# Eighteen extra products on TensorE in a hybrid attention and RWKV-7 layer

## The chip, the cores and the metric

The kernel runs on one core of a Trainium2 chip. The metric is the device time of one execution in microseconds (us). Three runs of the kernel before took 785.77, 785.54 and 783.43 us, median 785.54. One more execution was profiled.

The engines are named as the profile names them: PE is TensorE's matmul, PEld its weight load, DVE is VectorE, ACT is ScalarE, POOL is GpSimd and SP is SyncE, which here only issues DMAs. PEq, SPq and the like are the sequencers of the engines. Each engine has its own list of instructions; where one of them is not ready, the trace shows the engine idle and names what ended the wait.

## The reference, cut to what matters

One transformer layer, 512 tokens of width 1024, all in fp32:

```python
proj = rmsnorm(x, ln_mix_g) @ w_in                   # 1024 x 3096
y_nsa  = nsa_mixer(proj[..., :1304], ...)            # attention: compressed, selected, window branch
y_rwkv = rwkv7_mixer(proj[..., 1304:], ...)          # a recurrent scan over 512 tokens, 8 heads of 64
x = x + concatenate([y_nsa, y_rwkv]) @ w_out
hidden = square(relu(rmsnorm(x, ln_ffn_g) @ w_ff1))  # 1024 x 4096
x = x + hidden @ w_ff2
```

The attention has 8 query heads in two groups of four; each group shares one key head. There are only 8 selectable blocks and up to 16 are taken, so the selected branch is plain causal attention over all 512 tokens, and so is the window branch. The end of the RWKV mixer that the change touches is

```python
g = sigmoid(xg) @ g2          # the output gate
y = (y + bonus * v) * g
```

## The kernel before, in words

Tokens are cut in four blocks of 128, counted by `i`. Large products are done as three products of a high and a low part (`mm3`, lines 332 to 334), with both parts in the type fp32r. Small products are plain fp32; the profile shows each of those as two matmul records, so that four products read as x8.

The work has these stages. First the input projection (tiles `pa`) runs, about 20 to 225 us. Woven into its second half and going on after it is the RWKV mixer, per block: `rw_prep` (decays, gates, the products `pg` at L586 and the transposes `ptb` at L597), `rw_inv` (the inverse of a triangular matrix by many 32x32 products `pz`, `pd`, `px`), `rw_vals`, `rw_chain` (the scan itself, tiles `pp`, `puu`, `py`, two steps a block) and `rw_out` (group norm, transposes `pty` at L787, the gate product `pgt` at L797, then `YR`). From about 230 us the attention runs beside it in eight units: `UNITS` holds group 0 with blocks 0 to 3, then group 1. For a unit, `attn_scores` makes the compressed scores `pcs` (L1053), then for each of two branches the scores `sc` (L1075) of four heads in one to four PSUM banks. DVE reads each bank with a fused add, minimum and row minimum (L1079), ACT takes the exponential (L1082), and DVE, ACT or POOL scale by the reciprocal sum. `attn_values` transposes the probabilities (`pT`, L1111) and multiplies with the values (`pv`). After about 384 us come the output projection and the feed-forward part, in which PE has long runs of `mm3`.

Three things set the order around the change. The generators of the stages are merged by a small planner (`merge`) that takes, of those ready, the one of highest priority, with made-up costs and delays in the `yield` lines. Then the tile framework schedules the recorded instructions with a timeline of its own, so that an added instruction may move others on every engine. Last, PSUM buffers are shared: `ps` has one buffer, which `pg`, `ptb`, `pty`, `pgt` and others take in turn, and `pa` has two, which `pcs` and the banks of `sc` take in turn. A product into a new tile waits until the old one has been read.

Other names of the change and the prediction: `ident` is the 128x128 unit matrix, `G2P` the permuted gate weights (128 x 512, fp32), `SG` the gate's input, `Qt` a unit's transposed queries (128 x 512, fp32r), `KT` the transposed keys, `QR` and `rs_yq` the queries of a group before their transposition and the reciprocal roots of their norms (a power on POOL, L302), `QU` the last part of the inverse.

Of the kernel before, what the change touches and what calls it, by code (L numbers as in the profile page):

```python
# [50 lines left out]
UNITS = [(i, g) for g in range(2) for i in range(NT)]  # L51
# [63 lines left out]
def layer(ctx: ExitStack, tc: tile.TileContext, A, cst, out):  # L115
    nc = tc.nc
    PSUM = bass.MemoryType.PSUM
    V, S, G, PE = nc.vector, nc.scalar, nc.gpsimd, nc.tensor

    def bc(ap, shape):  # L120
        return ap.to_broadcast(shape)
# [54 lines left out]
    def at(place, shape, name, dt=F32):  # L176
        size, n = PLACES[place]
        assert int(np.prod(shape[1:])) * 4 <= size
        return up.tile(shape, dt, name=name, tag=place, bufs=n)
# [10 lines left out]
    def small(n, name):  # L190
        return sm.tile([128, n], F32, name=name, tag=name, bufs=1 if n == 32 else 2)
# [12 lines left out]
    ident = identr.bitcast(F32)  # L204
# [13 lines left out]
    for q in FQ:  # L218
# [9 lines left out]
        else:  # L228
            h = int(q[1])
# [57 lines left out]
    def vec(key, j=0, n=1):  # L287
        return VEC[:, VO[key] + j:VO[key] + j + n]
# [10 lines left out]
    def rsqrt(v, n, key, p=128):  # L299

        y = small(n, "rs_y" + key)[0:p]
        G.tensor_tensor(y, v, bc(MH[0:p], [p, n]), op=ALU.pow)  # L302
        return y
# [27 lines left out]
    def mm3(o_, l, r, first, last):  # L331
        PE.matmul(o_, l[0], r[0], start=first, stop=False)  # L332
        PE.matmul(o_, l[0], r[1], start=False, stop=False)  # L333
        PE.matmul(o_, l[1], r[0], start=False, stop=last)  # L334

    def norm_T(i, x_, gain, NH_, NL_, place, pool, raw=None):

        ss = small(2, "ss")
        tmp = [at(place, [128, 512], "nt") for _ in range(2)]
        for b in range(2):  # L340
            S.activation(tmp[b], x_[b], AF.Square, scale=1.0 / 32, accum_out=ss[:, b:b + 1])
        vv = small(1, "vv")
        V.scalar_tensor_tensor(vv, ss[:, 0:1], 1e-6, ss[:, 1:2], op0=ALU.add, op1=ALU.add)
        rs = rsqrt(vv, 1, 'n')
        for b in range(2):
            V.scalar_tensor_tensor(tmp[b], x_[b], rs, gain[b], op0=ALU.mult, op1=ALU.mult)
            pt = pool([128, 4, 128], "pt")
            for kk in range(4):
                PE.transpose(pt[:, kk, :], tmp[b][:, kk * 128:(kk + 1) * 128], ident)
            S.copy(NH_[b][:, i], pt)  # L350
            if raw:
                S.copy(raw[b], pt)
            V.tensor_tensor(NL_[b][:, i], pt, NH_[b][:, i].bitcast(F32), op=ALU.subtract)
# [22 lines left out]
    G2P = at('c', [128, 4, 128], "G2P")  # L376
# [392 lines left out]
    def rw_out(i):  # L769
        st = ST[i]  # L770
        YY = st['YY']
        mean = small(8, "mean")
        V.tensor_reduce(mean, YY, axis=AX.X, op=ALU.add)
        V.tensor_scalar(mean, mean, 1.0 / 64, None, op0=ALU.mult)
        V.tensor_tensor(YY, YY, bc(mean.unsqueeze(2), [128, 8, 64]), op=ALU.subtract)
        sq = at('o', [128, 8, 64], "sqy")
        S.activation(sq, YY, AF.Square)
        var = small(8, "var")
        V.tensor_reduce(var, sq, axis=AX.X, op=ALU.add)
        V.tensor_scalar(var, var, 1.0 / 64, 64e-5, op0=ALU.mult, op1=ALU.add)  # L780
        rs = rsqrt(var, 8, 'o')
        V.tensor_tensor(YY, YY, bc(rs.unsqueeze(2), [128, 8, 64]), op=ALU.mult)
        yield 0.0, 5.0
        pt = ps([128, 2, 2, 2, 64], "pty")
        for c in range(2):
            for p in range(2):
                PE.transpose(pt[:, c, p].rearrange("p a b -> p (a b)"),  # L787
                             YY[:, 4 * c + 2 * p:4 * c + 2 * p + 2, :].rearrange("p a b -> p (a b)"), ident)
        Y1 = at('o', [128, 4, 128], "Y1")
        for p in range(2):  # L790
            for e in range(2):
                S.activation(Y1[:, 2 * p + e, :].rearrange("p (c t) -> p c t", c=2), pt[:, :, p, 1 - e, :],
                             AF.Identity, bias=vec('lnb', 2 * p + e), scale=vec('lnw', 2 * p + e))
        G.tensor_tensor(Y1, Y1, st['ZV'], op=ALU.add)
        pgt = ps([128, 4, 128], "pgt")
        for kt in range(4):
            PE.matmul(pgt[:, kt, :], G2P[:, kt, :], SG[:, i * 128:(i + 1) * 128], start=True, stop=True)  # L797
        YR[i] = at('zk', [128, 4, 128], "YR")
        V.tensor_tensor(YR[i], Y1, pgt, op=ALU.mult)
        done['out', i] = 1  # L800
        yield 1.3, 0.0
# [8 lines left out]
    def rw_outs():  # L810
        for i in range(NT):
            yield lambda: ('chain', i) in done
            yield from rw_out(i)
# [10 lines left out]
    KT, VH, QT = {}, {}, {}  # L824
# [211 lines left out]
    def gate_over(z, g_):  # L1036
        V.reciprocal(z, z)
        V.tensor_tensor(z, z, g_, op=ALU.mult)  # L1038
# [5 lines left out]
    def attn_scores(i, g):  # L1044
        yield lambda: (UNITS.index((i, g)) < 2 or ('attn',) + UNITS[UNITS.index((i, g)) - 2] in done) and all(k in done for k in ('gates', ('cmp', 0), ('cmp', 1), ('keys', 0), ('keys', 1), ('q', i, g)))
        w = (i + 1) * 128
        hb = max(1, 512 // w) if w != 384 else 1
        gts = GT[:, i].rearrange("p (h b) -> p b h", b=3)[:, :, 4 * g:4 * g + 4]
        Qt = QT[i, g]

        pcs = pa_([128, 4, 32], "pcs")
        for h in range(4):
            PE.matmul(pcs[:, h, :], Qt[:, h, :].bitcast(F32), KCT[:, g, :], start=True, stop=True)  # L1053
        pc = at('cs', [128, 4, 32], "pcm")
        mnc = small(4, "mnc")
        zc = small(4, "zc")
        for h in range(4):
            V.tensor_tensor_reduce(out=pc[:, h], in0=pcs[:, h], in1=CT2[:, C_CD + 32 * i:C_CD + 32 * i + 32],
                                   scale=2.0 ** -(4 * g + h + 1), scalar=3e38,
                                   op0=ALU.add, op1=ALU.min, accum_out=mnc[:, h:h + 1])  # L1060
            S.activation(pc[:, h], pc[:, h], AF.Exp, bias=mnc[:, h:h + 1], scale=-1.0, accum_out=zc[:, h:h + 1])
        gate_over(zc, gts[:, 0])
        V.tensor_tensor(pc, pc, bc(zc.unsqueeze(2), [128, 4, 32]), op=ALU.mult)
        yield 0.9, 0.0

        P = []
        for br in range(2):
            P_ = at('n8', [128, 4, 512], "P")
            mn = small(4, "mn")
            z = small(4, "z")  # L1070
            for h0 in range(0, 4, hb):
                sc = pa_([128, hb, w], "sc")
                for h in range(h0, h0 + hb):
                    for hl in range(2):
                        PE.matmul(sc[:, h - h0, :], Qt[:, h, :],  # L1075
                                  KT[br, g, hl].rearrange("p i t -> p (i t)")[:, 0:w], start=hl == 0, stop=hl == 1)
                for h in range(h0, h0 + hb):
                    p_ = P_[:, h, 0:w]
                    V.tensor_tensor_reduce(out=p_, in0=sc[:, h - h0, :], in1=DIST[:, 512 - w:512],  # L1079
                                           scale=2.0 ** -(4 * g + h + 1), scalar=3e38,  # L1080
                                           op0=ALU.add, op1=ALU.min, accum_out=mn[:, h:h + 1])
                    S.activation(p_, p_, AF.Exp, bias=mn[:, h:h + 1], scale=-1.0, accum_out=z[:, h:h + 1])  # L1082
                yield SCP * hb * w / 512, SCD * hb * w / 512
            gate_over(z, gts[:, 1 + br])
            for h in range(4):
                if (h, br) in SCA:
                    S.activation(P_[:, h, 0:w], P_[:, h, 0:w], AF.Copy, scale=z[:, h:h + 1])
                else:
                    (G if (h, br) in SCG else V).tensor_scalar(P_[:, h, 0:w], P_[:, h, 0:w], z[:, h:h + 1], None, op0=ALU.mult)  # L1089
            P.append(P_)  # L1090
        pct = pb_([128, 128], "pct")
        PE.transpose(pct, pc.rearrange("p h n -> p (h n)"), ident)
        pcT = at('cs', [128, 128], "pcT")
        S.copy(pcT, pct)
        AT[i, g] = P, pcT
        yield 0.9, 0.0
        done['sc', i, g] = 1
# [335 lines left out]
```

## Time and profile before

| what | value |
|---|---|
| median of three runs (lowest, highest) | 785.54 us (783.43, 785.77) |
| profiled execution | 783.81 us |
| its span, first to last instruction | 781.9 us |
| PE, PEld busy | 759.8 us (97%), 657.5 us (84%) |
| DVE, ACT, POOL busy | 511.8 us (65%), 395.6 us (51%), 175.2 us (22%) |
| mean granted clock of TensorE | 0.987 of full speed |
| chain of waits: PE, DVE, ACT, DMA | 84%, 7%, 4%, 3% of the span |

The span is 1.9 us shorter than the execution's time; the rest lies before the first and behind the last instruction. [...]

### The profile page before, as it was taken

Reading aid. Unit: us, or ns where it says so; the run is one execution under the profiler, and the core shown is the slowest. Engines: PE = TensorE matmul, PEld = TensorE weight load, DVE = VectorE, ACT = ScalarE, POOL = GpSimd, SP = SyncE. Lnnn points to the kernel's source line nnn. Section 1 sums busy time; section 2 is a strip of 40 time slices with the busy share of each in tenths; the row PEclk is TensorE's granted clock in tenths of the full one; section 3 lists DMA queues with packets and bytes.
Section 4 is the critical chain, followed back from the end, with each engine's and each line's share of the span. In section 5 each row is a group of like instructions: output and inputs, shape, how many; then the busy total and the mean of one; then the engine's idle time right before and its main releaser. Section 6 shows DMA issues by size and latency. Waiting matters only on the chain.

```text
span 781.9 us, 18278 instructions
## 1 busy us (share of the span) xinstructions
PE 759.8 (97%) x7357; PEld 657.5 (84%) x7357; DVE 511.8 (65%) x1157; ACT 395.6 (51%) x928; POOL 175.2 (22%) x176
## 2 busy tenths in 40 slices
PE   7999999999989999999999899999999999999998
PEld 5888888889879877887788899998888999978886
DVE  6444385585586789898755888973334989853333
ACT  7343433345444867888544655673332456653330
POOL 5002032240332353434400152300001323100000
PEclk9999999999985999999999999999999999999999
DMA  7741331111000000120343053233323433133212
GB/s 235 206 133 42 94 84 44 44 29 31 15 16 1 29 3 2 30 57 9 114 149 95 17 146 108 69 104 110 96 92 103 118 102 106 62 122 95 95 54 108
DMA packets 67338, 62.00 MB, mean 79 GB/s; under 512 B 6013, under 2 KB 53299, under 8 KB 67254
## 3 DMA queue, kind: packets, MB, share of 16 engines
q1 hardware_dynamic: 67254, 60.83, 25.9%
q8 instruction: 58, 0.95, 0.5%
q14 instruction: 26, 0.21, 0.1%
HBM read 58.72 MB, written 2.10 MB: 78 GB/s over the span
## 4 chain that ended last, share of the span: by engine, by line
PE 84%; DVE 7%; ACT 4%; DMA 3%; issue 1%; SPq 1%; POOL 0%; DVEq 0%; ACTq 0%; POOLq 0%
PE pa L332 8%; PE pa L333 8%; PE pa L334 8%; PE po L332 7%; PE po L333 7%; PE po L334 7%; PE pw L333 5%; PE pw L334 5%; PE pw L332 5%; PE pg L586 2%; PE sc L1075 2%; DMA wraw<-in_w_out_dram 1%; PE py L757 1%; PE pT L1111 1%; PE pz L681 1%
## 5 line engine op out<-in xcount | busy, mean ns | idle before, releaser
L311 ACT CAST whi<-wraw 128x512 fp32r<-128x512 f32 (+1 forms) x128 | 78.7, 622 | 133.4 <-PE po L333 29.1
L312 DVE TENSOR_TENSOR wlo<-wraw,whi 128x512 fp32r<-128x512 f32 (+1 forms) x120 | 86.7, 725 | 86.1 <-ACT whi L311 80.9
L332 PE MATMUL po<-whi 128*128 128x512 f32 x256 | 100.7, 394 | 1.2 <-DVE cc L1361 1.2
L333 PE MATMUL po<-wlo,whi 128*128 128x512 f32 x256 | 101.0, 395 | 0.0
L334 PE MATMUL po<-whi,wlo 128*128 128x512 f32 x256 | 100.7, 393 | 0.0
L333 PE MATMUL pw<-TT,whi 128*128 128x256 f32 x224 | 63.2, 282 | 0.0
L334 PE MATMUL pw<-TT,wlo 128*128 128x256 f32 x224 | 63.0, 281 | 0.0
L332 PE MATMUL pw<-TT,whi 128*128 128x256 f32 x224 | 62.5, 279 | 0.0
L332 PEld LDWEIGHTS po<-whi 128*128 128x128 f32 x256 | 48.0, 188 | 13.0 <-ACT whi L311 1.6
L334 PEld LDWEIGHTS po<-whi,wlo 128*128 128x128 f32 x256 | 48.1, 188 | 11.4
L333 PEld LDWEIGHTS po<-wlo,whi 128*128 128x128 f32 x256 | 48.0, 188 | 11.0
L332 PE MATMUL pa<-XH,whi 128*128 128x512 f32 (+1 forms) x144 | 53.0, 372 | 1.5 <-ACT XH L350 1.5
L333 PE MATMUL pa<-XL,whi 128*128 128x512 f32 (+1 forms) x144 | 53.7, 374 | 0.0
L334 PE MATMUL pa<-XH,wlo 128*128 128x512 f32 (+1 forms) x144 | 52.9, 370 | 0.0
L1291 POOL TENSOR_TENSOR ws<-wq 128x512 f32<-128x512 f32 x14 | 21.5, 1536 | 138.3 <-DMA wq<-in_w_ff_dram 123.2
L311 ACT CAST whi<-ws 128x512 fp32r<-128x512 f32 x56 | 33.0, 617 | 34.7 <-DVE ws L1296 9.5
L312 DVE TENSOR_TENSOR wlo<-ws,whi 128x512 fp32r<-128x512 f32 x56 | 48.2, 870 | 3.1 <-ACT whi L311 3.0
L1089 POOL TENSOR_SCALAR P<-P,z 128x128 f32<-128x128 f32 (+3 forms) x32 | 36.1, 1138 | 60.8 <-DVE z L1038 28.5
L312 DVE TENSOR_TENSOR wlo<-H,whi 128x512 fp32r<-128x512 f32 x32 | 22.1, 690 | 42.1 <-PE po L333 37.4
L334 PE MATMUL pw<-NH,wlo 128*128 128x256 f32 x168 | 47.0, 280 | 0.0
L333 PE MATMUL pw<-NL,whi 128*128 128x256 f32 x168 | 46.8, 279 | 0.0
L332 PE MATMUL pw<-NH,whi 128*128 128x256 f32 x168 | 46.8, 279 | 0.0
(317 smaller groups left out, 2007.9 us busy)
## 6 DMA issues: line engine op xcount, KB each, us to landing
wraw<-in_w_ff_dram SPq DMA_DIRECT2D x72, 256.0 KB
wq<-in_w_ff_dram SPq DMA_DIRECT2D x56, 256.0 KB
wraw<-in_w_in_dram SPq DMA_DIRECT2D x40, 256.0 KB
wraw<-in_w_in_dram SPq DMA_DIRECT2D x8, 268.0 KB
x<-in_x_dram SPq DMA_DIRECT2D x8, 256.0 KB
y<-in_x_dram SPq DMA_DIRECT2D x8, 256.0 KB
wraw<-in_w_out_dram SPq DMA_DIRECT2D x8, 256.0 KB
wraw<-in_w_out_dram SPq DMA_DIRECT2D x16, 128.0 KB
```

The lines of the kernel that those rows point to most:

```text
L311: S.copy(hi, raw)
L312: eng.tensor_tensor(lo, raw, hi.bitcast(F32), op=ALU.subtract)
L332: PE.matmul(o_, l[0], r[0], start=first, stop=False)
L333: PE.matmul(o_, l[0], r[1], start=False, stop=False)
L334: PE.matmul(o_, l[1], r[0], start=False, stop=last)
L586: PE.matmul(pg[:, f], BK[ROW[e], 2 * f + c].rearrange("p a b -> p (a b)"), AR[c][ROW[e], f].rearrange("p a b -> p (a b)"), start=True, sto ...
L681: PE.matmul(o_[rows, b_, :], l[rows, b_, :], r[rows, b_, :], start=True, stop=True)
L757: PE.matmul(py[ROW[a], r, f, :], YL[e][c][:, f, a, :], uv, start=not q and f == 0 and e == 0, stop=True, skip_group_check=True)
L1075: PE.matmul(sc[:, h - h0, :], Qt[:, h, :], KT[br, g, hl].rearrange("p i t -> p (i t)")[:, 0:w], start=hl == 0, stop=hl == 1)
L1089: (G if (h, br) in SCG else V).tensor_scalar(P_[:, h, 0:w], P_[:, h, 0:w], z[:, h:h + 1], None, op0=ALU.mult)
L1111: PE.transpose(pt[:, h, :], P[br][:, h, j * 128:(j + 1) * 128], ident)
L1291: G.tensor_tensor(s3, q[0][0], q[1][0], op=ALU.subtract)
```

## The change

A helper `stir` issues a product several times into the same place. It is called twice: six products of the unit matrix with the gate weights (fp32, 512 columns) go into the bank of `pgt`, for block 0 only, ahead of the four gate products; and two products of keys with queries (fp32r, 512 columns) go into each score bank of the first two units, (block 0, group 0) and (block 1, group 0). Unit 0 has one bank a branch and unit 1 has two, so that is 2 x (2 + 4) = 12. Every such product is overwritten by the product that follows it, so nothing reads it.

```diff
+    def stir(o_, l, r, n):
+
+        for _ in range(n):
+            PE.matmul(o_, l, r, start=True, stop=True)
...
         pgt = ps([128, 4, 128], "pgt")
+        if i == 0:
+            stir(pgt, ident, G2P, 6)
         for kt in range(4):
             PE.matmul(pgt[:, kt, :], G2P[:, kt, :], SG[:, i * 128:(i + 1) * 128], start=True, stop=True)
...
                 sc = pa_([128, hb, w], "sc")
+                if UNITS.index((i, g)) < 2:
+                    stir(sc.rearrange("p h t -> p (h t)"), KT[br, g, 0][:, 0], Qt.rearrange("p h t -> p (h t)"), 2)
                 for h in range(h0, h0 + hb):
```

Lines behind the helper move by 5, behind the first call by 7 and behind the second by 9. The added products stand at line 339.

On PE, at the end of the input projection, the order before is:

```order
L333 MATMUL pa<-wlo,XH 128x256
L334 MATMUL pa<-whi,XL 128x256
L797 MATMUL pgt<-SG,G2P 128x128 x4
L702 MATMUL pz<-Tn,QU 32x32 x16
L1053 MATMUL pcs<-KCT,QT 128x32 x4
L1075 MATMUL sc<-KT,QT 128x128 x8
L586 MATMUL pg<-AR,BK 128x128 x4
L712 MATMUL px<-Tn,Z 32x32 x16
L1075 MATMUL sc<-KT,QT 128x128 x8
L1053 MATMUL pcs<-KCT,QT 128x32 x4
```

The same place on PE now:

```order
L333 MATMUL pa<-wlo,XH 128x256
L334 MATMUL pa<-whi,XL 128x256
L339 MATMUL pgt<-G2P,identr 128x512 x6
L804 MATMUL pgt<-SG,G2P 128x128 x4
L707 MATMUL pz<-Tn,QU 32x32 x16
L1060 MATMUL pcs<-KCT,QT 128x32 x4
L339 MATMUL sc<-QT,KT 128x512 x2
L1084 MATMUL sc<-KT,QT 128x128 x8
L591 MATMUL pg<-AR,BK 128x128 x4
L717 MATMUL px<-Tn,Z 32x32 x16
L339 MATMUL sc<-QT,KT 128x512 x2
L1084 MATMUL sc<-KT,QT 128x128 x8
```

Here only the added products came in; the order of the others is as it was. Some twenty instructions further on PE's order begins to differ in other ways too, up to about the output projection.

On DVE, right behind the products `rkp` and the last step of block 1's inverse, the order before is:

```order
L671 STREAM_TRANSPOSE Tn<-Tn 128x256
L715 TENSOR_SCALAR QU<-Tn,CT 128x8x32 x2
L799 TENSOR_TENSOR YR<-Y_2092,pgt 128x512
L953 TENSOR_REDUCE s_4455<-sqq 128x8
L1058 ISA pcm,mnc<-pcs,CT_171 128x32
```

The same place on DVE now:

```order
L676 STREAM_TRANSPOSE Tn<-Tn 128x256
L720 TENSOR_SCALAR QU<-Tn,CT 128x8x32
L960 TENSOR_REDUCE s_4461<-sqq 128x8 x2
L961 TENSOR_SCALAR s_4461<-s_4461 128x16
L806 TENSOR_TENSOR YR<-Y_2092,pgt 128x512
L964 TENSOR_TENSOR rs_yq<-rs_yq,CT_171 128x16
L720 TENSOR_SCALAR QU<-Tn,CT 128x8x32
L967 TENSOR_TENSOR QR<-QR,rs_yq 128x512 x2
L1065 ISA pcm,mnc<-pcs,CT_171 128x32
```

The normalisation of group 1's queries (the sums `s`, the roots `rs_yq` that POOL makes from them, and the scaling of `QR`) now stands ahead of the first read of the compressed scores `pcs`; before, it was spread over the next dozens of DVE's instructions.

## Rows read from the trace of the kernel before

**Rows 1.** The page's slices, one fortieth of the span each, TensorE's granted clock in tenths.

```profile
PEclk9999999999985999999999999999999999999999
```

**Rows 2.** Span and mean granted clock of the core.

```profile
core 0: 781.9 us, clock 0.987
```

**Rows 3.** Six stretches: length; busy time (instructions) of each engine; granted clock; DMA share, GB/s.

```profile
225.00:230.20 5.20, 2.07 (x43) 1.84 (x43) 5.10 (x10) 2.76 (x8) 2.89 (x2) 1.00 0.16 52
230.20:250.70 20.50, 20.50 (x164) 19.00 (x164) 12.56 (x65) 10.71 (x48) 5.37 (x5) 0.50 0.01 2
250.70:284.00 33.30, 33.30 (x672) 27.79 (x672) 27.15 (x93) 24.24 (x71) 13.22 (x16) 1.00 0.06 18
284.00:384.00 100.00, 95.22 (x1606) 77.59 (x1605) 90.41 (x289) 80.45 (x232) 42.71 (x36) 1.00 0.11 31
384.00:440.00 56.00, 55.40 (x283) 46.06 (x282) 33.07 (x54) 24.83 (x55) 7.72 (x8) 1.00 0.33 104
440.00:782.00 342.00, 334.86 (x2049) 297.47 (x2047) 218.16 (x362) 153.64 (x287) 46.32 (x31) 1.00 0.32 98
```

**Rows 4.** Timeline of PE at 225 us: start, us, instructions, idle before and releaser.

```profile
225.02 1.16 PE L797 MATMUL pgt<-SG,G2P 128*128 128x128 f32 x8 [0.20 <-ACT Y L792]
229.29 0.69 PE L702 MATMUL pz<-Tn,QU 32*32 32x32 f32 x32 [3.11 <-DVE Tn L694]
```

**Rows 5.** Chain of waits, pieces at half clock: start, us on the chain, what.

```profile
235.35 0.99 PE px L712 x32
...
239.90 2.00 PE pg L586 x8
241.90 1.05 PE puu L743 x16
...
246.31 1.05 PE py L752 x16
247.36 1.90 PE py L757 x32
```

**Rows 6.** Chain of waits, the same pieces at full clock.

```profile
299.75 0.62 PE px L712 x32
...
302.54 1.09 PE pg L586 x8
...
319.85 0.61 PE puu L743 x16
...
323.89 0.61 PE py L752 x16
...
365.02 1.08 PE py L757 x32
```

**Rows 7.** Chain of waits at 81 us: an fp32 product of 512 columns.

```profile
81.17 0.86 PE pu L534 x2
```

**Rows 8.** Timeline of PE at 384 us: fp32r products of 512 columns, back to back.

```profile
384.37 0.39 PE L333 MATMUL pa<-wlo,whi 128*128 128x512 f32 x1
384.60 0.40 PE L334 MATMUL pa<-whi,wlo 128*128 128x512 f32 x1
```

**Rows 9.** Timelines of POOL and DVE: the power, a sum, the queries' scaling, two waits for PE.

```profile
230.90 0.68 DVE L953 TENSOR_REDUCE s<-sqq 128x8 f32<-128x512 f32 x1
...
236.30 2.90 POOL L302 TENSOR_TENSOR rs_yq<-s,MH 128x16 f32<-128x16 f32 x1 [8.34 <-DVE zc L1037]
238.28 0.29 DVE L1079 CUSTOM_DVE_ANT_0 P<-sc,CT 128x128 f32<-128x128 f32 x1 [1.97 <-PE sc L1075]
...
245.04 1.29 DVE L960 TENSOR_TENSOR QR<-QR,rs_yq 128x512 f32<-128x512 f32 x2
...
249.31 0.42 DVE L763 TENSOR_TENSOR Sn<-py,Sn 128x256 f32<-128x256 f32 x1 [2.13 <-PE py L757]
```

**Rows 10.** A stretch of four us at 288 us, and PE's idle time in it.

```profile
288.00:292.00 4.00, 3.22 (x78) 2.45 (x79) 4.00 (x19) 3.13 (x12) 0.39 (x1) 1.00 0.00 2
288.48 0.73 PE L1075 MATMUL sc<-KT,QT 128*128 128x512 f32 x2 [1.11 <-DVE mnc L1058]
```

## The prediction

> **What bounds the kernel now.** I began with the granted clock. The core's mean is 0.987 [rows 2]; a kernel of which PE is busy 97% cannot be judged without it. The slices show where the missing part lies: all of it in two neighbouring slices of forty, marked 8 and 5, around 215 to 254 us [rows 1]. [...] So one fall of 20.5 us is the whole of it.
>
> Then I read what PE did before the fall. The gate products ended at 225.02 + 1.16 = 226.2 us, and PE stood idle for 3.11 us until DVE handed over the last step of an inverse at 229.29 us; what followed was 32x32 products [rows 4]. Within the fall PE is busy 20.50 of 20.50 us while DVE is busy 12.56 and ACT 10.71 [rows 3]: here PE's own pace sets everything, and DVE stands waiting for it, for instance 1.97 us before a score bank and 2.13 us before the scan's state [rows 9]. That changes later. From 284 to 384 us DVE is busy 90.41 of 100 us and PE has 4.8 us of idle time; from 384 us on PE is the bound, 55.40 of 56 and 334.86 of 342 us [rows 3]. That last part is as long whenever it starts. So the question is how much earlier the DVE-heavy stretch begins, and whether it keeps what it is given.
>
> **The change part by part.** It removes nothing. It adds 18 products to PE and, through the scheduler, moves instructions on all engines.
>
> *What a held clock gives.* I matched pieces of the chain of waits at half clock with the same pieces later at full clock: pg 2.00 and 1.09, px 0.99 and 0.62, puu 1.05 and 0.61, py 1.05 and 0.61, and 1.90 and 1.08 us [rows 5, 6]. Together 6.99 against 4.01, a ratio of 0.574. All 20.5 us of the fall are PE work on that chain, so at full clock they take 20.5 x 0.574 = 11.8 us: 8.7 us less. Bounds: px alone, the worst of the five, has 0.62 / 0.99 = 0.63 and gives 7.6; pg, the best, 0.545 and gives 9.3.
>
> *The six products ahead of the gate.* An fp32 product of 512 columns takes 0.86 us [rows 7]; six take 5.2. They wait for the bank that the gate products waited for (ACT's read of the transposed output), so they start at 225.02 and end at 230.2. The four gate products behind them take 1.16 us [rows 4] and end at 231.4; the small products of the inverse, which DVE has ready at 229.29, start then instead. Of 5.2 us, 3.1 fill the idle time and 2.1 are delay. What queues behind on PE is all of it: inverse, compressed scores, scores. On DVE only YR waits for the gate product. If the clock fell within them they would cost up to twice 0.86 each; I count none of that here.
>
> *The twelve products in the score banks.* Two fp32r products of 512 columns start 0.23 us apart [rows 8]: 12 x 0.23 = 2.8 us, all on the path as long as PE is the bound. Between zero (PE waits for a bank's reader at that point anyway) and 12 x 0.46 = 5.5 (at half clock) I take 2.8: the rows show PE busy without a gap where they stand.
>
> [...]
>
> *The moved instructions.* Group 1's query normalisation is now done by DVE ahead of its first read of the compressed scores. One of its steps waits for POOL's power, which takes 2.90 us [rows 9]; DVE, in order, can do nothing behind it but wait. Its two sums of 0.68 us [rows 9] stand behind the step that freed PE at 229.29 and two short ones, so they are ready for POOL at about 231.5; the power ends at about 234.5, and until then DVE has only YR to do, about as long as one sum: some 2.3 us idle. Then the 1.29 us scaling [rows 9] follows, and only then the reads that free the `pa` banks, so PE comes to a stop after its second round of products, by my count for 1 to 1.5 us. Against this, the same 1.3 us of scaling is gone from 245 us. From nothing (DVE has 20.50 - 12.56 = 7.9 us of slack in the fall) to the whole 2.9 + 1.3 = 4.2, I take 1.0. On SP a load of x is moved past two loads of w_out; it is issued a hundred us later, and I cost it at nothing, by the cover of the DVE-bound stretch; if that cover failed, a load that waits for its buffer would hold the loads behind it.
>
> *Sum.* 783.8 - 8.7 + 2.1 + 2.8 + 1.0 = 781.0 us for an execution like the profiled one, 2.8 us or 0.36% less. The bounds: 783.8 - 9.3 + 2.1 = 776.6 and 783.8 - 7.6 + 2.1 + 2.8 + 4.2 = 785.3 with the clock held. The median of the runs is 1.7 us above the profiled execution. A fall that lasts longer in some runs would make such a difference, and would be gone with the fall; or it has another cause and stays. I cannot tell and add half: 781.0 + 0.9 = 781.9, and since a shorter way through block 1's inverse (DVE's order brings it ahead of later scores) is more likely to help the scan than to harm it, I forecast 781.5.
>
> **The rivals.** A measurement of this kernel can tell about 0.3% from no change, 2.4 us: below 783.2 is faster, above 787.9 slower.
>
> *DVE takes the gain.* With PE twice as fast, DVE's 12.56 us and its stall become the pace of the stretch, and behind it DVE is already at 90% [rows 3]. For it: the 2.3 us stall, and DVE's 27.15 of 33.3 us up to 284. Against it: in the fall DVE waited for PE, and work it does earlier it need not do later. Then the 3 us that the sum leaves shrink to about one: 784.5.
>
> *The clock falls all the same, later.* The six products fill the one idle time there was, and then hand over to the same small products; at full clock these leave PE waiting for DVE, by my count 1 to 1.5 us at 236. If that brings the clock down for as long as before, the added products are a pure loss: 2.1 us of delay, and 12 x 0.46 = 5.5 at half clock, 785.5 + 7.6 = 793.1 at most, about 790 where part of it falls into DVE's stall. The point from which it decides: the fall must last so long that what is left of the 8.7 us does not pay for 2.1 + 2.8 + 1.0 = 5.9, that is over a third of its length, about 6.6 us. Against it: between 288 and 292 us PE was busy only 3.22 us with an idle time of 1.11 us, and the clock stayed at 1.00 [rows 10].
>
> *The scan runs ahead.* The chain inverse, scan, output of block 1 is begun sooner, the DVE stretch is better filled, and its 9.6 us of idle time shrink by some: 2 to 3 us more, about 778.5.
>
> *The change does not do what it says*: the products come too late, after the clock has fallen. They start at 225.02, right behind the last full-speed product, since the bank's release is the one that the gate products waited for; I count this with the second rival.
>
> **How the numbers follow.** The forecast has 0.60 (its own range 779.8 to 783.8), DVE takes the gain 0.19, the clock falls all the same 0.13, the scan runs ahead 0.08. Faster: all of the last, nine tenths of the first and a little of the second, 0.64. Slower: the third but for a short fall, 0.11. Same: 0.25. The range 778.0 to 786.0 holds all cases but the clock's fall and the far ends of the others.
>
> **What would show it.** Right: the clock's row has no slice under 9 around 230 us and a mean of 1.00; `pgt` is followed by `pz` at about 231.4 with no idle time; `pg` takes 1.09 us from its first; the first piece of the output projection's long run starts about 3 us sooner than 384. The stall would be seen as DVE waiting for POOL's power between 232 and 235. Wrong: a stretch of 0.50 anywhere, or a clock of 1.00 with the same 384 us, by which the gain would have been lost between 250 and 384 us.

## The result and the profile after

The changed kernel takes 793.58 us in the median of four runs (790.97 to 798.73); the kernel before, beside it, 785.65 (783.43 to 787.72). The ratio is 1.0099, interval [1.0072, 1.0127]: 1% slower, where 0.5% faster was forecast, and outside the range. Six more runs gave 1.0123 [1.0092, 1.0154]. The profiled execution took 790.97 us.

The first row to read is the page's row of the clock's slices, as [rows 1]:

```profile
PEclk9999999999999989999999999999999999999999
```

and the core's span and mean clock, as [rows 2]:

```profile
core 0: 788.9 us, clock 0.996
```

The two low slices of before are gone, and a shallower one stands later. Windows of the changed kernel, the stretches and columns of [rows 3], with the first seam moved to the end of the six products:

```profile
225.02:232.80 7.78, 7.58 (x89) 4.18 (x88) 7.65 (x11) 4.13 (x11) 5.28 (x4) 1.00 0.13 36
232.80:250.70 17.90, 17.24 (x227) 15.43 (x225) 14.81 (x76) 12.90 (x55) 5.29 (x5) 1.00 0.01 3
250.70:284.00 33.30, 33.30 (x750) 27.84 (x751) 24.26 (x82) 22.48 (x64) 15.90 (x17) 1.00 0.06 18
284.00:384.00 100.00, 92.17 (x1485) 75.31 (x1484) 87.70 (x285) 79.94 (x230) 42.20 (x36) 0.97 0.12 37
384.00:440.00 56.00, 54.40 (x256) 43.84 (x257) 28.64 (x48) 21.51 (x46) 3.78 (x5) 1.00 0.31 94
440.00:788.90 348.90, 341.57 (x2105) 304.03 (x2103) 223.49 (x371) 158.39 (x299) 49.23 (x33) 1.00 0.32 96
```

The clock is 1.00 where it was 0.50, as intended. Yet from 284 to 384 us PE is busy 92.17 instead of 95.22 us and DVE 87.70 instead of 90.41: the stretch that was to keep the gain got worse on both engines. PE's timeline at the added products, beside [rows 4]:

```profile
227.54 5.42 PE L339 MATMUL pgt<-G2P,identr 128*128 128x512 f32 x12 [0.20 <-ACT Y L797]
232.79 1.05 PE L804 MATMUL pgt<-SG,G2P 128*128 128x128 f32 x8
233.78 0.69 PE L707 MATMUL pz<-Tn,QU 32*32 32x32 f32 x32
...
237.89 0.69 PE L717 MATMUL px<-Tn,Z 32*32 32x32 f32 x32
239.20 0.73 PE L339 MATMUL sc<-QT,KT 128*128 128x512 f32 x2 [0.62 <-DVE mnc L1065]
```

The 3.11 us of idle time are filled: `pgt`, then `pz` at once. (The stage begins 2.5 us later than in [rows 4]; of the eighteen traces three begin it at 225.0 us and the others between 226.7 and 228.1, runs with and without the six products being in both groups.) But PE is idle for 0.62 us before the second score bank. DVE's timeline names the cause, the wait that the prediction expected:

```profile
237.06 0.18 DVE L964 TENSOR_TENSOR rs_yq<-rs_yq,CT 128x16 f32<-128x16 f32 x1 [2.42 <-POOL rs_yq L302]
```

The low slice, in windows of four us (compare [rows 10]):

```profile
284.00:288.00 4.00, 2.52 (x44) 1.93 (x43) 4.00 (x10) 2.03 (x5) 1.64 (x2) 1.00 0.03 8
288.00:292.00 4.00, 3.13 (x45) 2.87 (x46) 3.89 (x17) 2.69 (x12) 0.00 (x0) 0.54 0.00 0
292.00:296.00 4.00, 4.00 (x16) 2.82 (x16) 4.00 (x15) 1.03 (x2) 2.57 (x2) 0.60 0.02 4
```

and what PE waited for in it, from PE's timeline:

```profile
288.87 1.41 PE L591 MATMUL pg<-AR,BK 64*128 64x128 f32 x5 [1.99 <-DVE BK L573]
```

So a clock of 0.50 still came, in another idle time of PE: shorter windows have 1.00 up to 288.0 us, 0.83 from there to 288.5 and 0.50 up to 295. At 0.50, 0.83 over half a us is 0.17 us, so by this estimate the fall begins at about 288.3 us, 1.4 us into the 1.99. This run was the mildest of its four: the other three had mean clocks of 0.985 to 0.993 and took 792.6 to 798.7 us.

### The profile page after: what moved, and what is told of

Same layout as the page of the kernel before. It is cut to its first block, busy times and chain, and to the rows that moved or that the text cites. A ratio compares the mean times of both kernels' runs of the same rounds, so it can differ in the third digit from the quotient of the medians.

```text
span 788.9 us, 18334 instructions
## 1 busy us (share of the span) xinstructions
PE 764.8 (97%) x7381; PEld 659.0 (84%) x7381; DVE 509.5 (65%) x1157; ACT 396.6 (50%) x928; POOL 176.2 (22%) x176
## 4 chain that ended last, share of the span: by engine, by line
PE 77%; DVE 13%; ACT 4%; issue 2%; DMA 2%; POOL 1%; SPq 0%; ACTq 0%; DVEq 0%; POOLq 0%
PE pa L332 9%; PE pa L333 8%; PE pa L334 8%; PE po L332 7%; PE po L333 7%; PE po L334 7%; PE pw L333 4%; PE pw L334 4%; PE pw L332 4%; PE pg L591 2%; DVE wlo L312 2%; PE sc L1084 2%; DVE tl L1125 1%; DVE P L1088 1%; PE pd L686 1%
```

## The experiments

The change does two things: it adds 18 products, and it makes the scheduler put the old instructions in another order. To part them, a function `follow` chains each engine's instructions, SP's loads too, in the order of a written list, without a wait between engines. "Old order" is the list of the kernel before, "new order" that of the changed kernel; an added product stands right ahead of the instruction that it was written before (`ahead_`). Sixteen experiments were made in four groups, one of them (e9) the changed kernel once more; ratios are to the kernel before in the same group.

```diff
+def follow(tc, nc):
+    for e, text in ORDER.items():            # ORDER: one list for each engine
...
+        for k in seq:
+            for ins in ahead_.get(traced[e][k].name, []) + [traced[e][k]]:
+                if prev is not None:
+                    tc.add_manual_dep(ins, prev.name, mybir.DependencyInfo(
+                        mybir.DependencyClass.NoSync, mybir.DependencyReason.DATA), reason="order")
+                prev = ins
...
         layer(tc, args, cst, out)
+        follow(tc, nc)
```

**Products and order apart.** Four kernels: all products in the old order; none in the new; six alone and twelve alone in the old order.

```diff
+SIX, TWO = 6, 2      # e1, ORDER old     0, 0 for e2, ORDER new     6, 0 for e3 and 0, 2 for e4, ORDER old
...
-            stir(pgt, ident, G2P, 6)
+            stir(pgt, ident, G2P, SIX)
...
-                    stir(sc.rearrange("p h t -> p (h t)"), KT[br, g, 0][:, 0], Qt.rearrange("p h t -> p (h t)"), 2)
+                    stir(sc.rearrange("p h t -> p (h t)"), KT[br, g, 0][:, 0], Qt.rearrange("p h t -> p (h t)"), TWO)
```

> All 18 products, with every engine's other instructions held in the order of the kernel before. Order theory (the products are cheap, the order that the scheduler made around them costs the time): no long stretch at half clock near 230 us, about 781 us, 780 to 784. Product theory (18 products on PE and the delay that they hand on cost the time whatever the order): 788 to 793 us. Clock theory (the clock falls later all the same): 786 to 790 us with a fall after 235 us in the trace.

Measured: 781.83 us, 0.9935 [0.992, 0.995], mean clocks 0.997 to 1.000.

> The 18 products left out, every engine's other instructions held in the order of the changed kernel. Order theory: slower than the kernel before, 788 to 797 us, since the order stays and the clock falls near 230 us as before. Product theory: 784 to 786 us, as before.

Measured: 795.45 us, 1.0095 [1.0078, 1.0112], mean clocks 0.982 and 0.983.

> Only the six products ahead of the gate, the other instructions in the order of before. Order theory: 778 to 783 us if the six alone hold the clock, 786 to 788 us if it falls a little later. Product theory: about 2 us above before, 787 to 788 us.

Measured: 783.6 us, 0.9954 [0.9933, 0.9974]; the mean clock varies between 0.989 and 0.998, and the five runs at 0.997 and 0.998 took 780.4 to 782.3 us.

> Only the twelve products in the score banks, the other instructions in the order of before. The clock falls at 230 us, before the first of them. All theories: 785 to 791 us; 5.5 us above before if they run at half clock and do nothing else, near before or below if they bring the clock back sooner.

Measured: 789.61 us, 1.004 [1.0024, 1.0055]; the fall at 230 us is there as before (0.56 from 230.0 to 250.6 us).

e1 and e2 lie in the ranges of the order theory. The products do what they were meant to do: in the old order they win 0.65%. The new order by itself loses 0.95%. With the products it costs 1.0099 / 0.9935 = 1.0165, some 13 us. The list itself is not what makes e1 fast: e2 has one too and is slow. (The kernel before with its own order in a list was not run.) The windows of e1, for 230 to 250, 284 to 384 and 384 to 440 us:

```profile
230.20:250.70 20.50, 20.50 (x241) 17.51 (x240) 16.86 (x85) 11.71 (x51) 5.37 (x5) 1.00 0.05 15
...
284.00:384.00 100.00, 95.08 (x1545) 77.16 (x1535) 89.54 (x287) 79.04 (x228) 42.51 (x36) 1.00 0.11 34
384.00:440.00 56.00, 55.09 (x282) 45.18 (x281) 33.53 (x55) 25.90 (x58) 5.52 (x7) 1.00 0.33 100
```

PE keeps the 95 us of [rows 3] here, against 92.17 after.

**Where the order costs.** The new order up to some time, the old one from there.

```diff
+ORDER = new list for what had started before T in the trace after, then the old list   # T = 244, 250.6, 269, 300
```

> All 18 products. Every engine goes by the new order for what had started before 244 us in the trace after (the normalisation of group 1's queries ahead of the compressed scores, with DVE's wait for POOL's power), and by the old order from there. Theory 'starvation' (the loss comes from 256 to 269 us, where PE does the scan and the next inverse ahead of score banks and DVE runs dry): the wait at 235 us is made good by 250 us, ratio to the kernel before about 0.994, as the 0.9935 of the products in the old order. Rival 'the wait' (the 2.4 us that DVE waits for POOL's power, and what PE then waits, are never regained): about 3 us more, ratio 0.997. Rival 'later' (the loss comes from the order behind 300 us): 0.9935.

> As before, with the seam at 250.6 us: the new order up to the end of the second unit's first score bank and the scan step beside it, the old order from there. Starvation: 0.994 to 0.995. The wait: 0.997. Later: 0.9935.

> As before, with the seam at 269 us: the new order holds through the stretch in which DVE was busy 5.2 of 12 us (256 to 268). Starvation: about 6 us more than the products in the old order, ratio 1.001. The wait: 0.997 still. Later: 0.9935 still. The trace should show DVE busy 5 to 6 of 12 us between 256 and 268 as in the kernel after, if its order alone makes that.

> As before, with the seam at 300 us: the new order also holds where the clock fell in the profiled run of the kernel after (288 to 295 us). Starvation: 1.001 and, if the clock falls there again, 2 to 3 us more, 1.004. The wait: 0.997. Later: 0.994 (the loss only shows with the whole new order, 1.0099).

Measured: 787.4 us, 1.0002 [0.9984, 1.0021]; 788.69, 1.0005 [0.9984, 1.0027]; 788.67, 1.0026 [1.0008, 1.0044]; 789.65, 1.0032 [1.0013, 1.0051]. None of the three theories had that: 0.7% is lost by 244 us, little more up to 300, and as much again only with the rest. The clock column shows what all three had left out, falls of the clock, a fall being a stretch at 0.50. Windows of e6, columns as in [rows 3]:

```profile
236.00:240.00 4.00, 3.40 (x49) 3.01 (x49) 3.63 (x23) 2.50 (x13) 0.34 (x1) 0.89 0.01 2
240.00:244.00 4.00, 4.00 (x19) 3.94 (x20) 2.56 (x16) 3.69 (x17) 1.19 (x2) 0.50 0.00 2
244.00:248.00 4.00, 4.00 (x30) 3.40 (x28) 2.35 (x15) 2.15 (x11) 1.26 (x2) 0.50 0.00 0
248.00:252.00 4.00, 4.00 (x16) 3.52 (x16) 2.30 (x11) 2.67 (x8) 0.00 (x0) 0.50 0.00 0
252.00:256.00 4.00, 4.00 (x62) 3.45 (x61) 2.26 (x9) 1.59 (x6) 0.00 (x0) 0.90 0.02 4
```

PE's and DVE's timelines of e6 where the fall begins:

```profile
237.22 0.69 PE L719 MATMUL px<-Tn,Z 32*32 32x32 f32 x32
238.51 0.74 PE L341 MATMUL sc<-QT,KT 128*128 128x512 f32 x2 [0.60 <-DVE mnc L1067]
...
236.37 0.17 DVE L966 TENSOR_TENSOR rs_yq<-rs_yq,CT 128x16 f32<-128x16 f32 x1 [2.40 <-POOL rs_yq L304]
```

Behind the 0.60 us in which PE waits for DVE, which waits for POOL, the clock is at 0.50 for about 13.7 us (0.44 + 6.0 + 0.4 us lost, twice that at half). The twelve runs say the same: ten have a mean clock of 0.989 to 0.991 and take 787.7 to 789.8 us; two have 1.000 and take 780.0 and 783.8.

That gives a way to part the causes in all runs. A least-squares fit with a level for each kernel (its time carried to a mean clock of 1.00) and one slope on the mean clock, over the 220 runs whose clock is on record, has a slope of 6.1 us for each 0.01 of the clock and leaves 1.1 us (standard deviation). Fitted alone, the kernels whose clocks spread by 0.005 or more have slopes between 4.1 and 8.8. The levels: 777.8 us for the kernel before, 779.5 for e3, 780.9 for e4, 781.3 for e1, 782.3, 782.5, 784.3 and 782.7 for e5 to e8, 789.0 for the changed kernel with its ten runs, e9's among them. Those of the kernels whose clock always fell (before, e2, e4, e13, e14) are carried beyond their runs and are the less certain. By this, e1 and the changed kernel are 7.7 us apart by order and, at mean clocks of 0.9987 and 0.9899, 5.3 us by falls; e5 to e8 are only 1 to 3 us behind e1 by order, and the rest of what they lose is falls.

**The falls, tested.** The changed kernel once more; e6 with three more products in the first score bank, ahead of the idle time; the new order with these three and with three ahead of the `pg` at 288 us.

```diff
-                    stir(sc.rearrange("p h t -> p (h t)"), KT[br, g, 0][:, 0], Qt.rearrange("p h t -> p (h t)"), TWO)
+                    stir(sc.rearrange("p h t -> p (h t)"), KT[br, g, 0][:, 0], Qt.rearrange("p h t -> p (h t)"),
+                         TWO + (3 if (i, g, br, h0) == (0, 0, 0, 0) else 0))     # e10 and e11
...
                 pg = ps([128, 4, 2, 64], "pg")
+                if i == 3 and (c, e) == (0, 0):                               # e11 only
+                    stir(pg.rearrange("p f a b -> p (f a b)"), ident, G2P, 3)
```

> The changed kernel itself once more, for more runs with their clocks and a second trace. Theory 'two pieces' (in the runs so far a mean clock lower by 0.01 goes with about 6.2 us; carried to a clock of 1.00, the changed kernel takes about 788 us and the products in the old order 781, so the new order costs 7 us by itself and 5 us by falls of the clock): the runs lie on a line of 6 to 7 us for each 0.01 of the clock that ends near 788 at 1.00. Rival 'order alone': the times do not follow the clock.

Measured: 795.42 us, 1.0123; from 791.97 us at a clock of 0.997 to 799.83 at 0.984, a line of 6.0 us for each 0.01 that ends at 789.5: two pieces.

> The kernel with the new order to 251 us, with three more products in the first score bank of the first unit, where PE stood idle for 0.6 us behind DVE's wait for POOL's power; the clock fell right behind that place in the trace (from about 238.5, to 0.50). Theory 'the idle time brings the clock down': clock 0.998 or more in nearly all runs (0.990 without them in 10 of 12), about 782.5 us, ratio 0.995 instead of 1.0005. Rival 'the clock falls there for another reason': clock 0.990 as before, and 0.7 us more time.

Measured: 784.51 us, 0.9978 [0.9964, 0.9992]; mean clocks 0.997 to 1.000 in all twelve runs. The same place in the windows of e10:

```profile
236.00:240.00 4.00, 4.00 (x55) 3.50 (x55) 2.76 (x15) 1.63 (x9) 1.21 (x1) 1.00 0.01 2
240.00:244.00 4.00, 3.96 (x43) 3.63 (x42) 3.86 (x26) 3.93 (x20) 0.54 (x1) 1.00 0.00 0
```

and in PE's timeline of e10, the first bank's five products and the second bank's two:

```profile
235.49 1.41 PE L341 MATMUL sc<-QT,KT 128*128 128x512 f32 x5
...
239.38 0.73 PE L341 MATMUL sc<-QT,KT 128*128 128x512 f32 x2
```

The idle time is gone and so is the fall, so in e6 the fall came from this place. The three products both fill the idle time and give PE more work ahead of it, and which of the two holds the clock is not parted. The time is 2 us above what was expected.

> The changed kernel's own order, with the same three more products, and three (fp32, 512 columns) ahead of the first pg of block 3, where PE stood idle for 1.99 us at 287 us and the clock fell behind it. Two pieces: the clock stays at 0.998 or more, and the time is about 788.5 to 789.5 (788.3 and up to 1 us for the products), ratio 1.002 instead of 1.0099. Rival 'order alone': 793 or more.

Measured: 791.84 us, 1.0072 [1.0052, 1.0092], clock 1.000 in four runs of six (789.4 to 791.9 us). Between the two expectations. At a clock of 1.00 this kernel is 9.6 us behind e1 (790.9 by the line), of which the six products that fill (3 x 0.86 + 3 x 0.23 = 3.3 us by [rows 7, 8], part of it in idle time) are at most 3.3: the new order costs 6 us or more without any fall.

> All 18 products. The old order for what had started before 300 us in the trace of the products in the old order, the new order from there. Theory 'late' (at full clock the new order up to 300 us costs 1 to 3 us and behind 300 us the other 4 to 6, since there the last units' products are put behind the scan's and the attention ends later): 786 to 787 us at a clock of 0.998, ratio 0.999. Rival 'early' (the new order only costs by the stretch up to 300 us, where DVE runs dry): 781 to 782, ratio 0.9935.

Measured: 791.59 us, 1.0078 [1.0049, 1.0107]; 788.5 us carried to a clock of 1.00, 7 us above e1: "late", and more than expected. With e8, the same two lists the other way round, 1.4 us above e1, this says that most of what the order costs without a fall comes from behind 300 us.

**What the order does behind 284 us.** PE's waits from 284 to 402 us, total, times and longest; first e1, then the changed kernel, those of 0.6 us or more:

```profile
PE pv L1135 <- ACT th L1126: 1.7, 2, 1.2
PE sc L1086 <- DVE mnc L1067: 1.1, 1, 1.1
PE pv L1139 <- DVE tl L1127: 0.7, 1, 0.7
PE pp L743 <- DVE Sn L771: 0.6, 1, 0.6
```

```profile
PE pg L591 <- DVE BK L573: 2.0, 1, 2.0
PE pv L1137 <- DVE tl L1125: 1.9, 4, 0.7
PE pv L1133 <- ACT th L1124: 1.5, 2, 1.1
PE px L717 <- ACT Z L711: 1.0, 1, 1.0
PE pv L1133 <- ACT whi L311: 0.8, 1, 0.8
PE sc L1084 <- DVE mn L1088: 0.7, 1, 0.7
PE pp L741 <- DVE Sn L769: 0.6, 1, 0.6
```

With the smaller ones that the view lists, 4.8 us in e1 (4.9 in the kernel before) against 9.2. Timelines say what is late: the last unit's `pcT` (the transposed compressed scores, which end its scores), the last product with values `pv` and the scan's last `YR`; first e1, then the changed kernel:

```profile
366.53 0.27 ACT L1105 COPY pcT<-pct 128x128 f32<-128x128 f32 x1
394.73 0.39 PE L1139 MATMUL pv<-tl,VH 128*128 128x512 f32 x1
399.74 0.69 DVE L808 TENSOR_TENSOR YR<-Y,pgt 128x512 f32<-128x512 f32 x1
```

```profile
377.89 0.24 ACT L1103 COPY pcT<-pct 128x128 f32<-128x128 f32 x1
401.00 0.40 PE L1137 MATMUL pv<-tl,VH 128*128 128x512 f32 x1
388.52 0.67 DVE L806 TENSOR_TENSOR YR<-Y,pgt 128x512 f32<-128x512 f32 x1
```

The scan runs ahead by 11 us and the attention's last scores lag by 11. The other traces go by this too: with the old order behind 300 us (ten of the eighteen, those of the kernel before, e8 and e10 included) the last `pv` ends 4.6 to 5.4 us before the last `YR`, with the new order there (six) 12.2 to 14.8 us after it, and in the scheduler's own orders for e13 and e14, tried below, 3.1 and 7.9 us after it. The last scores then come when PE has little else to do, and each transpose and product waits for DVE's or ACT's part. The chain of waits on the profile pages says the same, first e1, then the changed kernel:

```profile
PE 84%; DVE 6%; ACT 5%; DMA 2%; issue 1%; SPq 0%; POOL 0%; ACTq 0%; DVEq 0%; POOLq 0%
PE 77%; DVE 13%; ACT 4%; issue 2%; DMA 2%; POOL 1%; SPq 0%; ACTq 0%; DVEq 0%; POOLq 0%
```

The long run of the output projection, which in e1 fills PE among the last values from 381.7 us on, begins 12 us later; first e1, then the changed kernel:

```profile
381.40 0.50 PE L1135 MATMUL pv<-th,VH 128*128 128x512 f32 x1 [1.21 <-ACT th L1126]
381.74 0.40 PE L336 MATMUL pa<-whi,wlo 128*128 128x512 f32 x1
```

```profile
390.86 0.50 PE L1133 MATMUL pv<-th,VH 128*128 128x512 f32 x1 [1.07 <-ACT th L1124]
...
393.81 0.40 PE L334 MATMUL pa<-whi,wlo 128*128 128x512 f32 x1
```

Of the 9.1 us between the two spans, 5.4 is idle time of PE behind 225 us (563.88 - 546.27 us against 554.80 - 542.54, length less busy time). That the lag is what costs the time is read from these views; no run moves it alone.

**This order, or any?** The scheduler's own order for six alone and for twelve alone; the new order from 345 us on; and the old order with one product in each bank.

```diff
+SIX, TWO = 6, 0     # e13, no list      SIX, TWO = 0, 2     # e14, no list
+ORDER = old list for what had started before 345 us in the trace of e1, then the new list   # e15
+SIX, TWO = 6, 1     # e16, old list
```

> The six products alone, in the order that the scheduler gives them (the same six in the old order: ratio 0.9954). It puts the queries' normalisation ahead of the compressed scores as the changed kernel does, and about a fifth of PE's products stand elsewhere than in the old order. Theory 'any reshuffled order loses' (the old order is a good one among those that the scheduler draws, and a new draw costs 5 to 8 us at full clock, beside the falls behind the idle time at 238 us): ratio 1.003 to 1.010. Rival 'this draw alone' (the loss belongs to the order of the whole change): 0.9954 to 0.999.

> The twelve products alone, in the scheduler's order (in the old order: 1.004, with the clock's fall at 230 us as in the kernel before). Here the queries' normalisation stays behind the compressed scores. Any reshuffled order loses: 1.010 to 1.014. This draw alone: 1.003 to 1.006.

> All 18 products, the old order up to 345 us in the trace of the products in the old order, the new order from there (from 300 us it cost 7 us at full clock, 788.4 against 781.3, with the attention's values some 9 us late from the unit at 305 us on). Theory 'scan ahead of attention between 300 and 345' (there the new order takes PE's and DVE's time for the scan, and the last units come late): at most 1 us left, 782 to 783, ratio 0.9945. Rival 'the end' (the order of the output projection and the last values costs it): 787 to 788.

> The old order with the six products and one instead of two in each score bank. By the runs so far twelve products cost 1.8 us at full clock (781.3 against 779.5 with six alone) and hold the clock (mean 0.9987 against 0.9932). If six hold it as well: 780.8, ratio 0.992. If the clock falls again in some runs: 782 to 783.6, 0.9935 to 0.9954.

Measured: 795.61 us, 1.0115 [1.0089, 1.014] for e13, six alone (0.9954 in the old order); 797.56, 1.0148 [1.0111, 1.0184] for e14, twelve alone (1.004); 797.41, 1.014 [1.0115, 1.0165] for e15; 781.15, 0.9926 [0.9899, 0.9952] for e16. So it is not one unlucky draw: three sets of products, three new orders, each 1.1 to 1.65% behind the old order with the same products. Not all of that is order alone: the mean clock is 0.983 in e13 against 0.993 in e3, and 0.977 in e14 against 0.9845 in e4, and by the levels (785.3 and 784.1 us) the order itself costs 6 and 3 us and falls the rest. e15 met neither expectation and is worse than either whole order, 792.2 us at a clock of 1.00. A likely reason, not shown, is that a seam between two lists leaves work of each in the wrong place. So what the seams of e5 to e8 and e12 cost by themselves isn't known, and the split by time is rough; how much of the order's 7.7 us arises before 345 us stays open. e16 has the lowest median of all and met the first of its expectations (the clock held, 0.997 or more in all six runs), but its interval holds e1's ratio, so that the two are not told apart.

## Why the prediction was wrong

- **What bounds the kernel**: right. One fall of the clock [rows 3], behind 3.11 us of PE's idle time [rows 4]; with the six products in it the clock is 1.00 there, from 230.2 to 250.7 us in e1 and from 232.8 to 250.7 in the changed kernel. The last part is as long whenever it starts, as was said: from the feed-forward part's first `pw` product to the end all eighteen traces take 321.3 to 323.3 us.
- **What a held clock gives, less the six products' delay**: 8.7 - 2.1 = 6.6 us. Six added to the twelve in the old order bring 0.9935 / 1.004 = 0.9895, 8.2 us; six alone 3.6 us in the mean, and 5 to 7 in the runs whose clock stayed at 0.997 or above. The size holds.
- **The twelve products**: 2.8 us. Alone they cost 0.4%, 3.1 us; at full clock on top of the six 781.3 - 779.5 = 1.8. They also pay something back: with them the mean clock is 0.9987, without 0.9932.
- **The moved instructions**, the step that failed: 1.0 us, bounds 0 and 4.2, against some 13 measured, three times the upper bound: 7.7 us of order and 5.3 of falls that come with it. The stall itself was foreseen well: DVE waited 2.42 us for POOL (2.3 predicted), PE 0.62 (1 to 1.5). But only this one place was priced. All that follows in the order, up to the output projection, was taken as nothing, or as help ("more likely to help the scan than to harm it"). The scan did run ahead, and that was the harm: the attention, which lags, ends last. Without this step the sum was 780.0, 3.8 us better than before; e1, which is the change without it, is 5.1 us better. The load of x moved on SP, put at nothing, did not cost, though it holds the loads behind it (it waits 66.5 us for POOL's `Y`, until 326.9 us, and SP issues nothing meanwhile): ACT waits 5.3 us for `w_out` between 340 and 420 us, against 11.9 in the kernel before and 12.7 in e1.
- **Half of the 1.7 us** by which the runs lay above the profiled one: a whole was due. Of the 82 runs of the kernel before, the 35 at the profiled run's clock (0.986 or 0.987) have a median of 785.5 us, so at the same clock the 1.7 us stays; the 43 at 0.984 or 0.985 have 787.7.
- **The clock falls all the same, later**: a rival with 0.13, and it came true for some 5 of the 13 us on the mean, but not at the place it named: in the changed kernel's two traces the clock fell at 288 and at about 394 us (e9: 0.93 from 390 to 394 us, 0.65 from 394 to 398), and held at 1.00 behind the idle time before the second score bank, 0.62 us in the first of them; in those of e5 to e8 it fell there, at 238 to 241 us (e6: 0.89 from 236 to 240 us, 0.50 from 240 to 252; mean clocks of the four traces 0.995, 0.990, 0.993 and 0.987). Where it fell in the runs with the lowest clocks, which have no trace, stays open. It was held low by one stretch in which 1.11 us of idle time passed without a fall [rows 10]. One such case doesn't clear the next. (Its "over a third" is 2.8 / 8.7 = 0.32, the 6.6 us that it gives.)
- **The scan runs ahead**: right in fact, wrong in sign. **DVE takes the gain**: DVE was less busy, not more, yet it is 13% of the chain instead of 7%. The order made that and not the held clock, since e1 has 6%.
- **What would show it**: the clock's row was named rightly as the view; the "wrong" sign came true, a stretch of 0.50 and a late output projection.

## What to carry to other kernels

Where a scheduler orders the program, an added instruction is two changes: pin the old order and time the product alone before judging it, since here the products won 0.65% and the reshuffle lost 1.65%. Compare when each chain's last result comes, not only busy shares: here the order in which attention and scan end some 5 us apart was the faster one, and the order in which the scan ends 12 us or more ahead the slower. Plot the runs' time against their mean clock: a line gives a first split of clock and order, surer where a kernel's clocks reach 1.00 and less so where it is carried there.

## What was not expected of the hardware

- An idle time of PE of 0.60 us (e6) was followed by about 13.7 us at half clock, while 0.62 us in the changed kernel's trace and 1.11 us [rows 10] were followed by none. In these three the length alone doesn't decide.
- In e6 the clock stayed at 0.50 through three windows of four us in which the records show PE busy 4.00 of 4 us, and in the kernel before for 20.5 us at 20.50 [rows 3].
- The start of the same stage differs by some 2 to 3 us between traces (225.0 us in three, 226.7 to 228.1 in fifteen), though the kernel before (225.0), e1 (227.0) and e4 (227.1) have PE's instructions in the same order up to there.
